# An attention stage's hand-written order: two query chunks moved ahead of an output projection, the first two heads' groups scored one step later

## The chip, the cores and the metric

One core of a Trainium2 chip. The metric is the device time of one execution in microseconds; the median of several runs counts. A difference under about 0.2% of it is small for the scatter of these runs.

## What is computed

One layer of a decoder trunk on 256 positions of 2048 features: a normalized input goes through one input projection; an SSD (Mamba-2) group and an attention group work side by side; one output projection adds both to the residual stream h; a gated feed-forward part and an embedding gate follow. The change lies in the attention group and in the output projection:

```python
a = rmsnorm(h)
z, xbc, dt, q, k, v = split(a @ W_in)          # 2048 -> 8224
...                                            # y_ssm from z, xbc, dt
qh, kh = rope(rmsnorm(q)), rope(rmsnorm(k))    # 32 query heads, 8 key heads of 64
for blk in blocks_of_128(positions):           # keys: this block and the one before
    sc = qh[blk] @ kh[blk-1:blk+1].T * 64**-0.5, masked to a window of 128
    m  = max(max(sc), sink)
    pr = exp(sc - m) / (sum(exp(sc - m)) + exp(sink - m))
    y_att[blk] = pr @ v[blk-1:blk+1]
h = h + concat(y_ssm, y_att) @ W_out           # 4096 -> 2048
h = h + (silu(g) * u) @ W_down                 # g, u from a causal convolution of rmsnorm(h) @ W_up
h = h + sigmoid(rmsnorm(h) @ W_pg) * rmsnorm(p @ W_pe)
```

## The kernel before

All large matrix products run in float32 accuracy from split operands: each weight tile `w` (128 x 2 x 512 floats) is loaded by SP's DMA queue, ScalarE (ACT) casts it to a rounded `wh` (L192), VectorE (DVE) subtracts to get the rest `wl` (L193), and TensorE (PE) makes three products for each 128-row piece: L222 (hi x wh), L223 (hi x wl), L224 (lo x wh). There are seven buffers of `w` and four each of `wh` and `wl`. One such tile with both blocks of 128 positions is 12 matmuls; this is one *step*, counted by `slot` in the attention stage.

In the attention stage (L638 to L839) the order of PE's instructions is written out by hand; the other engines' queues are ordered by a planner that follows the program order and a simulated time. The parts are:

- `chunk(c, then)` (L791): one chunk of 512 columns of the input projection, 8 steps. After the last, `then` takes the accumulator: `keys` for chunk 10, `load_v` for chunk 11, `queries(j, ...)` for chunk 12 + j, named `q(j)`.
- `queries(j)` (L696): for each block of 128 positions, `norm_rope` (L663; ACT scales and squares, DVE reduces and multiplies, POOL takes the root and rotates), then `flipped` (L683): POOL copies the two 16-bit halves into `half` (L701), a transposing DMA on SP's queue writes `flip` (L688), POOL copies `flip` into the tile `qT` (L689). A `q(j)` holds the queries of 8 heads.
- `scores(j, b, kvs)` (L727): PE multiplies `qT` with `kT` into `sc` (L738), DVE adds the band mask (L742) and reduces to the maximum (L749), ACT takes the exponentials (L753), and the probabilities are divided (for block 0 by DVE, L763, for block 1 by ACT, L761) and transposed by the same `flipped` (ACT fills `half` at L765, POOL writes `s` at L689). Three calls serve one j: block 0, and block 1 for each of two key heads. `sc` has one buffer, `s1` (block 1) has three.
- `values(j)` (L769): PE multiplies probabilities and `v`; ACT and DVE split the result into a tile `y`, which becomes the left operand of `output(4 + j)`. `y` has three buffers.
- `output(i)` (L800): one 512-row piece of the output projection: four column groups of two steps. After each group DVE adds the two accumulators to h (`add_to_h`, L396). `output(1)` to `output(3)` serve the SSD group, 4 to 7 the attention group.

`half` and `flip` have two buffers each, `qT` has two for each block, and the accumulators two pairs. The dictionary `at` says after which step each call of scores and values is put; the tuple of parts (L823 to L833) says in what order the 8-step parts run. So the steps of the old order are: 0 to 7 keys, 8 to 15 q(0), 16 to 23 load_v, 24 to 31 q(1), 32 to 39 output(1), 40 to 47 q(2), 48 to 55 output(2), 56 to 63 q(3), 64 to 71 output(3), then output(4) to output(7) up to 103.

Of the kernel before, what the change touches and what calls it, by code (L numbers as in the profile page):

```python
# [65 lines left out]
def hybrid_layer(  # L66
# [54 lines left out]
    def acc_pair():  # L121
        return [ps_acc.tile([P, NC], F32, tag=f"acc{b}", name=nm(f"acc{b}")) for b in range(NB)]
# [17 lines left out]
    def load_first(k, pieces=1):  # L140

        xt = sb(xin, [P, T], "xt", bufs=6)
        nc.sync.dma_start(xt, xT[:, k, :])
        w = sb(wp, [P, KW, NC], "w", bufs=WR)
        n = KW // pieces
        for c in range(0, KW, n):
            cs = slice(c, c + n)
            nc.sync.dma_start(w[:, cs, :], w_in[cs, k // KW, :, (k % KW) * NC : (k % KW + 1) * NC].rearrange("c p n -> p c n"))
        return w, xt

    first = [load_first(0, KW), load_first(1, KW)]
# [46 lines left out]
    def load_w(src, kt=KW, pieces=1):  # L198

        w = sb(wp, [P, KW, NC], "w", bufs=WR)  # L200
        wh = sb(wp, [P, KW, NC], "wh", F32R)
        wl = sb(wp, [P, KW, NC], "wl", F32R)
        n = kt * NC // pieces
        w2, wh2, wl2 = (t.rearrange("p a b -> p (a b)") for t in (w, wh, wl))
        for i in range(pieces):
            s = slice(i * n, (i + 1) * n)
            nc.sync.dma_start(w2[:, s], src[:, s])
            split(w2[:, s], wh2[:, s], wl2[:, s])
        return wh, wl

    def products(acc, lhs, w, k0, kt, total, apart=False, halves=False, whole=None):

        wh, wl = w
        order = [(i, b) for i in range(kt) for b in range(NB)]
        if apart:
            order.sort(key=lambda ib: ib[1])
        if halves:
            order = order[:kt]
        for i, b in order:
            k = k0 + i  # L220
            hi, lo = lhs(k, b)
            PE.matmul(acc[b], lhsT=hi, rhs=wh[:, i, :], start=(k == 0), stop=False)  # L222
            PE.matmul(acc[b], lhsT=hi, rhs=wl[:, i, :], start=False, stop=False)  # L223
            PE.matmul(acc[b], lhsT=lo, rhs=wh[:, i, :], start=False, stop=(k == total - 1 or (b == NB - 1 and k + 1 == whole)))  # L224
        if halves:
            b = NB - 1
            for c in range(0, NC, NC // 2):
                cs = slice(c, c + NC // 2)
                for i in range(kt):
                    hi, lo = lhs(k0 + i, b)  # L230
                    for left, right in ((hi, wh), (hi, wl), (lo, wh)):
                        PE.matmul(
                            acc[b][:, cs],
                            lhsT=left,
                            rhs=right[:, i, cs],
                            start=False,
                            stop=True,
                            skip_group_check=True,
                        )
# [8 lines left out]
    class Lhs:  # L248
# [8 lines left out]
        def part(self, k):  # L257
            h, l = self.t[k // KG]
            return h[:, k % KG, :], l[:, k % KG, :]
# [133 lines left out]
    def add_to_h(acc, n):  # L393
        for b in range(NB):
            hs = hres[b][:, n * NC : (n + 1) * NC]
            V.tensor_tensor(out=hs, in0=hs, in1=acc[b], op=ALU.add)  # L396
# [241 lines left out]
    with tc.tile_pool(name="att_s", bufs=2) as as_, tc.tile_pool(name="att", bufs=2, reuse_waits="tile") as ap_, tc.tile_pool(name="ps_sc", bufs=1, space=PSUM) as ps_sc:  # L638
# [57 lines left out]
        def queries(j, acc):  # L696
            qTs[j] = []
            for b in range(NB):
                n = norm_rope(acc, b, qrope)
                qT = sb(ap_, [P, 4, P], f"qT{b}")  # L700
                flipped(qT, NC, lambda half: G.tensor_copy(half, halves(n)))  # L701
                qTs[j].append(qT)
# [66 lines left out]
        def values(j):  # L769

            yT = Lhs(yp_, KG, "y")
            for b in range(NB):
                o = tr_tile()
                for kv in range(2):
                    pT = probs.pop((j, b, kv))
                    vs = slice((2 * j + kv) * HD, (2 * j + kv + 1) * HD)
                    for kb in range(b + 1):
                        for e in range(2):
                            PE.matmul(  # L779
                                v3(o[e * HD : (e + 1) * HD, kv * 2 * P : (kv + 1) * 2 * P], 2),  # L780
                                lhsT=v[kb][:, vs],
                                rhs=pT[e][:, :, kb, :],
                                start=(kb == 0),
                                stop=(kb == b),
                                skip_group_check=True,
                            )
                hi, lo = (t[:, :, b * P : (b + 1) * P] for t in yT.t[0])
                split(v3(o, 4), hi, lo)
            held[4 + j] = (yT, w_out, 4 + j, 1)

        def chunk(c, then):  # L791
            acc = acc_pair()
            n = KT // KW
            for s in range(n):
                products(acc, aT, load_w(w_in[c, s]), s * KW, KW, KT, s == n - 1)
                if s == n - 1:
                    then(acc)
                yield

        def output(i):  # L800
            lhs, w, i0, ni = held.pop(i)
            for n in range(4):
                acc = acc_pair()
                for s in range(2):
                    products(acc, lhs, load_w(w[i0 * 2 + s, n]), s * KW, KW, KG, s == 1)
                    if s == 1:
                        add_to_h(acc, n)
                    yield

        at = {}  # L810
        for j, first, value in ((0, (28, 31, 34), 48), (1, (43, 46, 50), 64), (2, (58, 61, 65), 79), (3, (75, 77, 80), 93)):
            for n, (b, kvs) in zip(first, ((0, (0, 1)), (1, (0,)), (1, (1,)))):
                at[n] = lambda j=j, b=b, kvs=kvs: scores(j, b, kvs)
            at[value] = lambda j=j: values(j)
# [3 lines left out]
        def q(j):  # L818
            return chunk(12 + j, lambda acc: queries(j, acc))

        slot = 0
        with tc.manual_schedule(engines={PE.engine}):
            for part in (  # L823
                lambda: chunk(10, keys),
                lambda: q(0),
                lambda: chunk(11, load_v),
                lambda: q(1),
                lambda: output(1),
                lambda: q(2),
                lambda: output(2),  # L830
                lambda: q(3),
                *(lambda i=i: output(i) for i in range(3, 8)),
            ):  # L833
                for _ in part():
                    if slot in at:
                        at[slot]()
                    slot += 1
# [163 lines left out]
```

## Time and profile before

| | us |
|---|---|
| runs | 1432.59, 1432.73, 1434.25 |
| median | 1432.73 |
| the profiled execution | 1436.61 |
| its span, first to last instruction | 1434.9 |
| PE busy | 1423.2 (99%) |
| DVE busy | 984.1 (69%) |
| ACT busy | 804.2 (56%) |
| POOL busy | 286.2 (20%) |

The profile gives each engine's busy time, the idle time before each instruction with what ended it, and a timeline. A matmul's record is longer than the distance to the next matmul's start, so neighbouring records overlap, and holes are read from the starts. The granted TensorE clock is full (1.00) for the whole span.

### The profile page before, as it was taken

The numbers are of one execution on the slowest core, as the hardware profiler recorded it, in microseconds if no ns is written. First come the engines' busy times: TensorE is split into PE (matmuls) and PEld (weight loads), VectorE is DVE, ScalarE is ACT, GpSimd is POOL, SyncE is SP. The second block draws the span as 40 slices with busy tenths as digits, with TensorE's granted clock in tenths as the row PEclk, the third lists the DMA queues.
The fourth block names the chain that finished last, engine by engine and source line by source line (L and its number), as shares of the span: only waits on it lengthen the run. The fifth ranks groups of instructions, "written<-read, shape, count | busy, mean of one in ns | idle before, by whom it ended". The sixth has DMA issues, their size and how long they took to land.

```text
span 1434.9 us, 18092 instructions
## 1 busy us (share of the span) xinstructions
PE 1423.2 (99%) x6527; PEld 1167.3 (81%) x6527; DVE 984.1 (69%) x1242; ACT 804.2 (56%) x1101; POOL 286.2 (20%) x212
## 2 busy tenths in 40 slices
PE   9999999999999999999999999999999999999998
PEld 7887888888787778888888888888888888888887
DVE  6678876776678897656667646765675576476854
ACT  6675555644567666556556446545554554455643
POOL 0002010008345432013243112201320131120000
PEclk9999999999999999999999999999999999999999
DMA  9656656548687778577887767867876877776671
GB/s 332 236 173 198 215 177 185 171 148 223 188 220 187 209 220 220 168 211 207 219 226 202 217 205 206 225 196 198 230 208 192 223 201 218 206 208 190 208 226 65
DMA packets 163467, 292.62 MB, mean 204 GB/s; under 512 B 93041, under 2 KB 95921, under 8 KB 162993
## 3 DMA queue, kind: packets, MB, share of 16 engines
q1 hardware_dynamic: 162944, 290.99, 70.5%
q8 instruction: 51, 0.84, 0.2%
q10 hardware_dynamic: 432, 0.48, 0.1%
q14 instruction: 40, 0.32, 0.1%
HBM read 268.32 MB, written 2.13 MB: 188 GB/s over the span
## 4 chain that ended last, share of the span: by engine, by line
PE 68%; DVE 1%; ACT 0%; issue 0%; POOL 0%; DVEq 0%; ACTq 0%
PE acc L222 22%; PE acc L224 22%; PE acc L223 22%; PE tr L779 1%; PE tr L272 0%; PE sc L738 0%; DVE wl L193 0%; ACT s L753 0%; DVE nm L749 0%; DVE s L742 0%; ACT wh L192 0%; DVE sg L931 0%; ACT s L761 0%; DVE qkr L672 0%; DVE h L396 0%
## 5 line engine op out<-in xcount | busy, mean ns | idle before, releaser
L193 DVE TENSOR_TENSOR wl<-w,wh 128x1024 fp32r<-128x1024 f32 (+1 forms) x495 | 634.9, 1288 | 378.5 <-ACT wh L192 376.4
L192 ACT CAST wh<-w 128x1024 fp32r<-128x1024 f32 (+1 forms) x495 | 514.8, 1045 | 480.7 <-PE acc L224 431.4
L223 PE MATMUL acc<-wl,ah 128*128 128x512 f32 x1278 | 500.1, 391 | 1.5 <-DVE wl L193 1.5
L224 PE MATMUL acc<-wh,al 128*128 128x512 f32 x1278 | 499.0, 391 | 0.0
L222 PE MATMUL acc<-wh,ah 128*128 128x512 f32 x1278 | 498.3, 392 | 0.0
L223 PEld LDWEIGHTS acc<-wl,ah 128*128 128x128 f32 x1278 | 240.1, 188 | 52.3 <-DVE wl L193 2.4
L222 PEld LDWEIGHTS acc<-wh,ah 128*128 128x128 f32 x1278 | 240.1, 188 | 51.0 <-issue 1.4
L224 PEld LDWEIGHTS acc<-wh,al 128*128 128x128 f32 x1278 | 240.1, 188 | 50.1 <-issue 0.7
L224 PE MATMUL acc<-wh,gl 128*128 128x512 f32 x352 | 137.1, 390 | 0.0
L223 PE MATMUL acc<-wl,gh 128*128 128x512 f32 x352 | 137.1, 390 | 0.0
L222 PE MATMUL acc<-wh,gh 128*128 128x512 f32 x352 | 136.5, 390 | 0.0
L881 POOL COPY half<-u 128x1024 uint16<-128x1024 uint16 x44 | 62.0, 1422 | 264.3 <-ACT u L879 264.3
L222 PE MATMUL acc<-wh,yh 128*128 128x512 f32 x256 | 101.6, 397 | 0.6 <-DVE h L396 0.6
L223 PE MATMUL acc<-wl,yh 128*128 128x512 f32 x256 | 99.9, 390 | 0.0
L224 PE MATMUL acc<-wh,yl 128*128 128x512 f32 x256 | 99.7, 390 | 0.0
L884 POOL COPY uc<-flip 128x1024 uint16<-128x1024 uint16 x44 | 54.9, 1248 | 177.2 <-DMA flip<-half 174.9
L223 PEld LDWEIGHTS acc<-wl,gh 128*128 128x128 f32 x352 | 66.1, 188 | 13.7
L224 PEld LDWEIGHTS acc<-wh,gl 128*128 128x128 f32 x352 | 66.1, 188 | 13.6
L222 PEld LDWEIGHTS acc<-wh,gh 128*128 128x128 f32 x352 | 66.1, 188 | 13.6
L288 DVE SCALAR_TENSOR_TENSOR cv<-uc,fcw,cv 128x254 f32<-128x254 f32 (+1 forms) x176 | 73.2, 476 | 3.4 <-ACT cv L286 3.4
L396 DVE TENSOR_TENSOR h<-h,acc 128x512 f32<-128x512 f32 x112 | 73.0, 678 | 1.8 <-PE acc L224 1.8
L222 PEld LDWEIGHTS acc<-wh,yh 128*128 128x128 f32 x256 | 48.1, 188 | 14.6 <-issue 2.0
(239 smaller groups left out, 1129.2 us busy)
## 6 DMA issues: line engine op xcount, KB each, us to landing
w<-in_w_up_dram SPq DMA_DIRECT2D x176, 512.0 KB, 4.2
w<-in_w_in_dram SPq DMA_DIRECT2D x126, 512.0 KB, 4.2
w<-in_w_down_dram SPq DMA_DIRECT2D x88, 512.0 KB, 4.3
w<-in_w_out_dram SPq DMA_DIRECT2D x64, 512.0 KB, 4.2
w<-in_w_pg_dram SPq DMA_DIRECT2D x32, 512.0 KB, 4.3
seg<-scr SPq DMA_DIRECT2D x8, 512.0 KB, 5.0
xt<-in_xT_dram SPq DMA_DIRECT2D x16, 128.0 KB, 7.0
h<-in_x_dram SPq DMA_DIRECT2D x2, 1024.0 KB, 8.7
```

The lines of the kernel that those rows point to most:

```text
L192: S.copy(hi, src)
L193: V.tensor_tensor(out=lo, in0=src, in1=hi.bitcast(F32), op=ALU.subtract)
L222: PE.matmul(acc[b], lhsT=hi, rhs=wh[:, i, :], start=(k == 0), stop=False)
L223: PE.matmul(acc[b], lhsT=hi, rhs=wl[:, i, :], start=False, stop=False)
L224: PE.matmul(acc[b], lhsT=lo, rhs=wh[:, i, :], start=False, stop=(k == total - 1 or (b == NB - 1 and k + 1 == whole)))
L288: V.scalar_tensor_tensor(out=dst[:, s:], in0=ps[:, : T - s], scalar=taps[n - 1 - s], in1=dst[:, s:], op0=ALU.mult, op1=ALU.add)
L396: V.tensor_tensor(out=hs, in0=hs, in1=acc[b], op=ALU.add)
L779: PE.matmul(v3(o[e * HD : (e + 1) * HD, kv * 2 * P : (kv + 1) * 2 * P], 2), lhsT=v[kb][:, vs], rhs=pT[e][:, :, kb, :], start=(kb == 0), st ...
L881: G.tensor_copy(half.rearrange("p (a n) -> p a n", a=2), u_.bitcast(U16).rearrange("p (n a) -> p a n", a=2))
L884: G.tensor_copy(uc[:, :, b * P : (b + 1) * P].bitcast(U16).rearrange("p f (t a) -> p f t a", a=2), flip.rearrange("p (a f) t -> p f t a", ...
```

## The change

The order of the parts is altered: `q(2)` runs ahead of `output(1)` and `q(3)` ahead of `output(2)`; before, each ran behind it. The steps after which scores and values are put are altered with it.

```diff
-        for j, first, value in ((0, (28, 31, 34), 48), (1, (43, 46, 50), 64), (2, (58, 61, 65), 79), (3, (75, 77, 80), 93)):
+        for j, first, value in ((0, (29, 32, 35), 49), (1, (44, 47, 51), 65), (2, (58, 61, 66), 79), (3, (73, 75, 80), 93)):
...
                 lambda: q(1),
+                lambda: q(2),
                 lambda: output(1),
-                lambda: q(2),
-                lambda: output(2),
                 lambda: q(3),
-                *(lambda i=i: output(i) for i in range(3, 8)),
+                *(lambda i=i: output(i) for i in range(2, 8)),
```

In the new order q(2) has the steps 32 to 39, output(1) 40 to 47, q(3) 48 to 55 and output(2) 56 to 63; the rest stands as it was.

## Rows read from the trace of the kernel before

**Rows 1.** Page, busy us (share of the span) and instructions of each engine.
```profile
PE 1423.2 (99%) x6527; PEld 1167.3 (81%) x6527; DVE 984.1 (69%) x1242; ACT 804.2 (56%) x1101; POOL 286.2 (20%) x212
```

**Rows 2.** Waits of PE, whole run: who waited for whom, us, times, longest.
```profile
PE sc L738 <- POOL qT L689: 2.6, 2, 1.4
...
PE acc L222 <- DVE h L396: 0.6, 1, 0.6
```

**Rows 3.** Timeline of PE, steps 28 and 31: start us, us, instruction, [idle before <-releaser].
```profile
369.51 0.39 PE L224 MATMUL acc<-wh,al 128*128 128x512 f32 x1
...
370.19 0.39 PE L224 MATMUL acc<-wh,al 128*128 128x512 f32 x1
371.95 0.60 PE L738 MATMUL sc<-kT,qT 64*128 64x128 f32 x6 [1.37 <-POOL qT L689]
...
381.13 0.39 PE L224 MATMUL acc<-wh,al 128*128 128x512 f32 x1
381.44 1.13 PE L738 MATMUL sc<-kT,qT 64*128 64x256 f32 x8
```

**Rows 4.** Timeline of PE at the end of step 61.
```profile
474.61 0.39 PE L224 MATMUL acc<-wh,al 128*128 128x512 f32 x1
476.23 0.49 PE L738 MATMUL sc<-kT,qT 64*128 64x256 f32 x2 [1.24 <-POOL qT L689]
```

**Rows 5.** Timeline of PE in step 54, in output(2).
```profile
451.10 0.40 PE L224 MATMUL acc<-wh,yl 128*128 128x512 f32 x1
452.09 0.50 PE L222 MATMUL acc<-wh,yh 128*128 128x512 f32 x1 [0.59 <-DVE h L396]
```

**Rows 6.** Timeline of POOL, copies for queries(0) and queries(2) and one of scores.
```profile
370.75 1.15 POOL L689 COPY qT<-flip 128x1024 uint16<-128x1024 uint16 x1 [7.14 <-DMA flip<-half]
...
458.48 2.04 POOL L701 COPY half<-qkr 128x1024 uint16<-128x1024 uint16 x1
475.03 1.15 POOL L689 COPY qT<-flip 128x1024 uint16<-128x1024 uint16 x1 [14.51 <-PE acc L224]
476.80 2.91 POOL L689 COPY s<-flip 128x2048 uint16<-128x2048 uint16 x1 [0.62 <-DMA flip<-half]
```

**Rows 7.** Timeline of SP's DMA queue, 457 to 472 us.
```profile
459.65 9.34 SPq L207 DMA_DIRECT2D w<-in_w_out_dram  x5
469.08 5.55 SPq L688 DMA_TRANSPOSE flip<-half  x2
```

**Rows 8.** Groups of ACT, 356.8 to 560 us: count | busy, mean ns | idle before, releasers.
```profile
L765 ACT COPY half<-s 128x2048 uint16<-128x2048 uint16 x12 | 22.8, 1899 | 5.0 <-DMA flip<-half 2.8 <-DVE s L763 1.9 <-ACT wh L192 0.3
```

**Rows 9.** Timeline of DVE, steps 53 and 54, and at step 62.
```profile
450.23 1.21 DVE L749 TENSOR_REDUCE nm<-s 128x4 f32<-128x1024 f32 x1
451.36 0.67 DVE L396 TENSOR_TENSOR h<-h,acc 128x512 f32<-128x512 f32 x1
...
477.62 4.31 DVE L193 TENSOR_TENSOR wl<-w,wh 128x1024 fp32r<-128x1024 f32 x2
```

**Rows 10.** Windows: us, then busy of PE, PEld, DVE, ACT, POOL; output(1), q(2), output(2).
```profile
382.50:405.70 23.20, 23.20 (x107) 18.75 (x106) 21.80 (x30) 16.27 (x35) 14.16 (x13) 1.00 0.68 191
405.70:430.10 24.40, 24.40 (x122) 19.57 (x121) 16.29 (x20) 16.32 (x32) 7.95 (x4) 1.00 0.98 250
430.10:457.10 27.00, 26.41 (x130) 19.96 (x128) 24.32 (x33) 18.48 (x35) 15.18 (x13) 1.00 0.76 172
```

**Rows 11.** Groups of DVE, 356.8 to 560 us, columns as in rows 8.
```profile
L742 DVE TENSOR_TENSOR s<-sc,band 128x1024 f32<-128x1024 f32 x12 | 14.6, 1215 | 0.2 <-PE sc L738 0.2
...
L763 DVE TENSOR_TENSOR s<-s,den 128x1024 f32<-128x1024 f32 x4 | 4.9, 1222 | 0.1
```

**Rows 12.** Timeline of DVE, weight casts for the steps 57 and 58.
```profile
458.34 1.28 DVE L193 TENSOR_TENSOR wl<-w,wh 128x1024 fp32r<-128x1024 f32 x1 [0.75 <-ACT wh L192]
...
460.66 1.21 DVE L193 TENSOR_TENSOR wl<-w,wh 128x1024 fp32r<-128x1024 f32 x1
```

**Rows 13.** Timeline of PE, first matmul of step 57 that reads wl.
```profile
460.14 0.39 PE L223 MATMUL acc<-wl,ah 128*128 128x512 f32 x1
```

## The prediction

> **What bounds the kernel now.** I read the page first. TensorE (PE) is the engine that sets the time: it is busy for 99% of the span [rows 1]. A busy share of 99% still hides short holes, because a matmul's record (0.39 us) is longer than the distance to the next one's start (three take 0.68 us, so 0.227 each) [rows 3]. So the second view is the list of what PE waited for in the whole run. Only two entries lie in the attention stage that the change touches: 2.6 us in two waits of score matmuls for qT, and 0.6 us in one wait of an output-projection matmul for an addition to h [rows 2]. The third view is PE's timeline at these three places. It says how long each hole is from start to start, and this is what the change can give back. A step (12 matmuls) takes 12 x 0.227 = 2.72 us.
>
> The first hole is ahead of the first scores (step 28): 370.19 to 371.95 is 1.76 us, where the same hand-over three steps later (381.13 to 381.44) takes 0.31, so 1.45 us are lost [rows 3]. The second is ahead of the third query chunk's second scores (step 61): 474.61 to 476.23, 1.62 us, so 1.31 are lost [rows 4]. The third is in output(2), step 54: 0.99 us where 0.23 is usual, so 0.76 are lost [rows 5].
>
> The rule of the Trainium skill, "Perfetto Trace Analysis", section "Tensor Engine Instruction", is that a matmul's recorded end is modelled and not observed. The idle times of the rows (1.37, 1.24, 0.59) come from such ends and would put the first two holes at 2.61 us; start to start gives 2.76. I use the starts.
>
> **The change, part by part.** *First scores one step later (28 to 29, 31 to 32, 34 to 35).* Their qT copy ends at 370.75 + 1.15 = 371.90 [rows 6]. Queries(0) and everything in program order ahead of step 28 stay where they are, so I leave that time alone. The scores would now start at 370.19 + 2.72 + 0.31 = 373.22, with 1.3 us to spare. The hole of 1.45 us goes. What is late next is the second block's qT for step 32, which also gets one step more.
>
> *Third query chunk q(2) one output sooner (its last step goes from 47 to 39).* Its scores stay at 58 and 61. Today the second block's 16-bit copy is done at 458.48 + 2.04 = 460.52, but qT is copied only at 475.03 [rows 6]. The time between goes on SP's queue: five weight loads stand ahead of the two transposing DMAs, which are issued from 469.08 [rows 7]. Those loads cannot be passed; but 8 steps more (21.8 us) stand against a shortage of 1.31 us, so even an equally slow path is in time. This hole goes too. The sum so far is 1.45 + 1.31 = 2.76 us.
>
> *Fourth query chunk q(3) one output sooner (63 to 55), its scores at 73 and 75 (75 and 77 before).* It had no wait before and gets 6 steps more. Gain 0. What it costs is that all that queries() issues comes earlier: per chunk four ACT operations, six on VectorE (DVE), fourteen on POOL, and two transposing DMAs on SP. They go ahead of 8 weight loads on SP and 8 pairs of weight casts on ACT and DVE. The matmuls and weight loads of q and output only swap places, and are of equal size; PE's work is unchanged.
>
> *Values one step later (48 to 49, 64 to 65), scores 65 to 66.* values(0) writes the y buffer that output(1) reads, and output(1) now ends at step 47 rather than 39. Step 48 lies between, so this costs nothing; if that cover went, ACT's split would wait for the rest of a step, at most 2.72 us, and no matmul needs it before output(4). scores at 66 take the buffer that values(1) frees at 65, the same distance of one step as before. values(2) stays at 79, so its last scores have 13 steps rather than 14; there is no wait to judge from, so it is bounded by 0 and 2.72 us. I take 0, as the rows show no wait of a value matmul at 14 [rows 2].
>
> *A shared buffer.* The 16-bit copies of queries and scores rotate through two buffers. The scores at 44 and 47 now follow queries(2), and those at 58 and 61 follow queries(3), so ACT may have to wait for a transposing DMA. The nearest row: 2.8 us of such waiting in twelve copies, none of it followed by a PE wait [rows 8, 2]. Bounds 0 and 2.8; I take 0.
>
> *DVE, stage by stage.* This is where the third hole comes from, and it may come back. In output(2) the reduction of a score (450.23) sits on DVE's queue between the two additions to h, and the second addition starts at 451.36 and frees the accumulator at 452.03 [rows 9]. DVE is busy 21.80 of 23.20 us in output(1), 24.32 of 27.00 in output(2), but only 16.29 of 24.40 in q(2) [rows 10]. From the durations a block-1 score costs DVE 1.22 us for the band [rows 11] and 1.21 for the reduction [rows 9], 2.43 together, and a block-0 score 1.22 more for its multiplication [rows 11]; the small operations are left out on both sides. After the change output(1) follows queries(2) and holds one block-0 score in place of two block-1 scores: 21.80 - 4.86 + 3.65 = 20.6 us, in 23.2 less one score's 1.2 on PE, 22.0. Output(2) follows queries(3) and holds a block-0 and a block-1 score, where the old output(1) held two block-1: 21.80 + 1.22 = 23.0 in 23.2. So output(1) gets easier, and output(2) stays as tight as the old output(1), which had no wait, and tighter than the old output(2), which had one. I can't read from this whether the wait for h returns. Its price is between 0 and a few times 0.76; I take one such wait of the same size, because output(2) remains the stage with the least room. So nothing is gained on that hole: sum 2.76 us.
>
> **How the sum stands to the runs.** The profiled execution took 1436.61 us (span 1434.9), 3.9 above the median of 1432.73. Taking 2.76 off gives 1433.9 for a profiled execution and 1430.0 for the median. The holes might be a little shorter in an execution without the profiler; no row shows that.
>
> **Rivals.** *B: the third hole goes as well.* For it: the scores at 50 and the values at 48, which crowded DVE beside the additions, are no longer in output(2); output(1) gets lighter. Against it: 23.0 of 23.2. It gives 2.76 + 0.76 = 3.52 us less, 1429.2.
>
> *C: output(2) becomes DVE-bound, and the kernel ends slower.* Place: steps 56 to 63. There the weight casts run just ahead of PE: in the old run at the same steps a cast ended at 458.34 + 1.28 = 459.62 and the matmul that reads it started at 460.14, a lead of 0.52 us [rows 12, 13]. Price: two casts that started at 477.62 beside a POOL copy (476.80 for 2.91) took 4.31 us, where two at 1.21 take 2.42; 1.9 are lost [rows 6, 9, 12]. Moving queries(3) next to this stage puts four more POOL copies there. From a lead below 1.9 each such meeting stops PE for what is left. One or two of them give 1430.0 + 1.9 to 1430.0 + 3.8, 1431.9 to 1433.8. Three or more fully uncovered, 5.7 us and up, give 1435.7 or more: slower by over 0.2%. Against it: the total load on the stage before it (q(3), by the row of q(2)) leaves DVE 8 us to get ahead again, and the old output(1) met the same copies without a wait.
>
> The Trainium skill speaks against the change here: "SBUF — State Buffer", section "SBUF: two separate sides", calls the port pair that DVE and GpSimd share an exclusive lock, held for a whole instruction. The two casts above agree with it: the first would start when the POOL copy ends. By it alone rival C would be likelier than I make it.
>
> *D: the change doesn't reach the first wait.* The planner that orders SP's queue could put the transposing DMA one weight load later; qT would then be ready at 371.90 + 2.72 = 374.62, 1.4 after the scores could start, and the gain falls to 1.36: 1431.4. Against it: nothing ahead of step 28 in program order is altered.
>
> **How the numbers follow.** Forecast A (two holes gone, one stays), 1430.0: 0.40, its own range 1429.6 to 1430.4. B, 1429.2: 0.36. C: 0.12 for 1431.9 to 1433.8, and 0.07 for 1435.7 and more. D, 1431.4: 0.05. About 0.2% (2.87 us, so 1429.86 and 1435.60) is what a measurement here can tell from no change. B and a fifth of A are faster: 0.44. C's upper part is slower: 0.07. The rest, 0.49, is within. For 8 in 10 the range runs from 1428.9, a little under B, to 1432.9, which takes in D and half of C's lower part; C's upper half and a rest are left out.
>
> **What would show it.** In the new trace PE's list of waits should have no score matmul waiting for qT, with the hand-over at step 29 at 0.3 us; the second qT copy of the third chunk should end tens of us ahead of its scores. A wait for h, if any, should lie in steps 56 to 66. The forecast is wrong if PE waits for wl there (C), if the qT wait is still there (D), or if a hole opens outside the attention stage, which this reasoning leaves at zero.

## The result, and the profile after

| | before | after |
|---|---|---|
| median, us | 1433.63 (1432.59 to 1434.69, 8 runs) | 1437.69 (1437.09 to 1440.27, 8 runs) |
| the profiled execution, us | 1436.61 | 1437.09 |
| the attention stage in it, us | 312.47 | 314.77 |
| granted clock, mean of the span | 1.000 | 0.998 |

The ratio is 1.0032, with a 95% interval of 1.0021 to 1.0042: the change makes the kernel 4.06 us slower, where the forecast had it 2.7 us faster. The attention stage is counted here and below in the profiled execution from the last matmul of the SSD part to the last transposition of h, start to start; behind it both traces take the same time (817.94 and 817.93 us). Ahead of it the profiled execution of before lost 1.3 us more at weight casts than the one of after, and its stage began 1.8 us later. So the two profiled executions differ by 0.5 us only, the stage by 2.3, and the medians by 4.1; the 1.8 between the last two are not accounted for by one profile of each.

The engines' busy times, as in [rows 1], show nothing of it:

```profile
PE 1424.0 (99%) x6527; PEld 1167.3 (81%) x6527; DVE 984.1 (69%) x1242; ACT 803.8 (56%) x1101; POOL 282.3 (20%) x212
```

The waits of PE after, as in [rows 2]: no score matmul waits for qT any more. New is the first line, 3.4 us of waiting for ACT's copies of the accumulators of the queries (L665); the wait for h is still there.

```profile
PE acc L222 <- ACT qkr L665: 3.4, 2, 2.8
...
PE acc L222 <- DVE h L396: 0.5, 1, 0.5
```

PE's timeline after (start us, us, instruction, idle before and its releaser), at the first scores (step 29), then in output(1), steps 41 and 42, then at the start of step 58 in output(2), then in step 70 in output(3):

```profile
371.12 0.39 PE L224 MATMUL acc<-wh,al 128*128 128x512 f32 x1
371.44 1.16 PE L738 MATMUL sc<-kT,qT 64*128 64x128 f32 x16
...
408.33 0.39 PE L224 MATMUL acc<-wh,yl 128*128 128x512 f32 x1
411.47 0.63 PE L222 MATMUL acc<-wh,yh 128*128 128x512 f32 x1 [2.75 <-ACT qkr L665]
411.90 0.63 PE L223 MATMUL acc<-wl,yh 128*128 128x512 f32 x1
...
414.46 0.63 PE L223 MATMUL acc<-wl,yh 128*128 128x512 f32 x1
414.89 0.50 PE L224 MATMUL acc<-wh,yl 128*128 128x512 f32 x1
415.22 0.39 PE L222 MATMUL acc<-wh,yh 128*128 128x512 f32 x1
...
462.68 0.39 PE L224 MATMUL acc<-wh,yl 128*128 128x512 f32 x1
463.71 0.50 PE L222 MATMUL acc<-wh,yh 128*128 128x512 f32 x1 [0.65 <-ACT qkr L665]
...
504.77 0.50 PE L222 MATMUL acc<-wh,yh 128*128 128x512 f32 x1 [0.50 <-DVE h L396]
```

The first pair is the hand-over that took 1.76 us [rows 3]; it takes 0.32. The second hole [rows 4] is gone as well. In their place PE stands still at step 42 from 408.33 to 411.47, 3.14 us, of which 0.23 are usual: 2.91 lost. Behind that hole matmuls start 0.43 us apart (411.47, 411.90) rather than 0.227, which is half the rate: up to 415.22 there are eight such distances and one of 0.33, so 8 x 0.20 + 0.10 = 1.7 us more. At step 58 another 0.80 are lost (1.03 less 0.23), at step 70 0.66 in a wait for h. The sum is 2.91 + 1.7 + 0.80 + 0.66 - 1.45 - 1.31 - 0.76 = +2.55 us, against 2.30 measured for the stage.

What held the accumulator is seen on ACT's timeline after. The two copies L665, of q(2)'s two blocks, lie 3.8 us apart:

```profile
405.29 1.71 ACT L761 ACTIVATE s<-s,den 128x256 f32<-128x256 f32 x4 [0.76 <-DVE den L758]
406.91 0.67 ACT L665 ACTIVATE qkr<-acc,rx 128x512 f32<-128x512 f32 x1
407.48 1.89 ACT L765 COPY half<-s 128x2048 uint16<-128x2048 uint16 x1
409.27 1.04 ACT L192 CAST wh<-w 128x1024 fp32r<-128x1024 f32 x1
410.21 0.63 ACT L667 ACTIVATE hsq<-qkr 128x512 f32<-128x512 f32 x1
410.74 0.67 ACT L665 ACTIVATE qkr<-acc,rx 128x512 f32<-128x512 f32 x1
```

In the kernel before the two copies of q(1) and the two of q(2) follow each other closely:

```profile
382.84 1.26 ACT L665 ACTIVATE qkr<-acc,rx 128x512 f32<-128x512 f32 x2
...
432.04 0.68 ACT L665 ACTIVATE qkr<-acc,rx 128x512 f32<-128x512 f32 x1
432.74 0.63 ACT L667 ACTIVATE hsq<-qkr 128x512 f32<-128x512 f32 x1
433.28 0.67 ACT L665 ACTIVATE qkr<-acc,rx 128x512 f32<-128x512 f32 x1
```

Output(1) uses q(2)'s pair of accumulators for its second column group, from step 42 on. After the change PE could have gone on there at 408.56, and the second copy ends at 411.41. From 405.29 ACT has work without a pause until then: the division and the 16-bit copy of a block-1 score, a weight cast, a square. The windows after, q(2) and output(1) (columns as in [rows 10], the last three being granted clock, DMA share and GB/s; the third stretch lies in the second):

```profile
378.10:402.40 24.30, 24.30 (x113) 19.24 (x112) 20.35 (x26) 18.10 (x43) 11.19 (x8) 1.00 0.61 152
402.40:430.20 27.80, 25.05 (x113) 19.80 (x112) 23.27 (x26) 17.73 (x23) 20.18 (x21) 0.94 0.89 227
405.00:416.00 11.00, 8.25 (x30) 6.34 (x29) 7.58 (x10) 10.41 (x14) 5.00 (x4) 0.84 0.90 201
```

Over a whole stage ACT is busy 18.10 of 24.30 and 17.73 of 27.80 us, which looks like room; in the 11 us from 405 it is busy 10.41. But this share by itself doesn't make PE wait: in the kernel before ACT is busy for the whole 11 us from 376. The granted clock is 0.84 in the 11 us from 405.

### The profile page after: what moved, and what is told of

Read it like the earlier page. It is cut to its first block, busy times and chain, and to the rows that moved or that the text cites. A ratio compares the mean times of both kernels' runs of the same rounds, so it can differ in the third digit from the quotient of the medians.

```text
span 1435.3 us, 18092 instructions
## 1 busy us (share of the span) xinstructions
PE 1424.0 (99%) x6527; PEld 1167.3 (81%) x6527; DVE 984.1 (69%) x1242; ACT 803.8 (56%) x1101; POOL 282.3 (20%) x212
## 4 chain that ended last, share of the span: by engine, by line
PE 64%; DVE 0%; ACT 0%; issue 0%; DVEq 0%
PE acc L222 21%; PE acc L223 21%; PE acc L224 21%; PE tr L272 0%; PE tr L779 0%; PE sc L738 0%; DVE sg L930 0%; DVE wl L193 0%; DVE nm L749 0%; DVE s L742 0%; DVE sg L931 0%; ACT wh L192 0%; ACT s L761 0%; DVE h L396 0%; ACT sg L929 0%
```

## The experiments

Each group of experiments was timed beside the kernel before on one chip; rows with the same time under "before" are one group, and rows of different groups are compared by their distance from it. How far one schedule scatters between groups is seen at e15, which only moves tiles of after in memory: it is 3.0 us above its before, where after is 4.06 above. A difference of 1 us between groups is therefore not read. Stage is the attention stage of one profiled execution.

| | median, us | before | ratio (95%) | stage, us |
|---|---|---|---|---|
| before | | | | 312.47 |
| after | 1437.69 | 1433.63 | 1.0032 (1.0021 to 1.0042) | 314.77 |
| e1 scores of j = 0 later, alone | 1431.55 | 1433.95 | 0.9981 (0.9973 to 0.9990) | 309.53 |
| e2 after, those scores early | 1436.19 | 1433.95 | 1.0017 (1.0008 to 1.0025) | 313.97 |
| e3 q(2) moved, q(3) not | 1438.43 | 1433.95 | 1.0030 (1.0019 to 1.0041) | 317.23 |
| e4 q(3) moved, q(2) not | 1431.83 | 1433.95 | 0.9991 (0.9979 to 1.0002) | 310.40 |
| e12 e4, last scores later | 1432.02 | 1434.42 | 0.9983 (0.9974 to 0.9992) | 311.42 |
| e6 scores of j = 0 and 2 later | 1432.99 | 1434.17 | 0.9992 (0.9983 to 1.0001) | 310.82 |
| e7 before, a hole made | 1436.79 | 1434.17 | 1.0017 (1.0008 to 1.0026) | 314.56 |
| e5 after, third accumulator pair | 1435.50 | 1434.17 | 1.0008 (1.0000 to 1.0017) | 313.99 |
| e8 after, one copy by DVE | 1436.54 | 1434.17 | 1.0013 (1.0004 to 1.0022) | 314.53 |
| e10 after, a division left out | 1435.97 | 1434.42 | 1.0013 (1.0004 to 1.0022) | 313.96 |
| e11 after, a division without its wait | 1438.88 | 1434.42 | 1.0031 (1.0019 to 1.0042) | 317.00 |
| e13 e8 and e10 together | 1438.12 | 1434.51 | 1.0027 (1.0017 to 1.0038) | 314.43 |
| e14 after, three buffers qkr | 1437.16 | 1434.09 | 1.0019 (1.0011 to 1.0028) | 314.12 |
| e15 the room of e14 alone | 1437.09 | 1434.09 | 1.0020 (1.0011 to 1.0029) | 313.71 |
| e16 e14 and e5 together | 1437.46 | 1434.09 | 1.0029 (1.0019 to 1.0038) | 314.26 |
| e17 after, half of q(2)'s casts | 1433.40 | 1434.43 | 0.9994 (0.9985 to 1.0003) | 311.33 |
| e18 e1, half of q(2)'s casts | 1431.71 | 1434.43 | 0.9980 (0.9971 to 0.9989) | 308.56 |

### Which part of the change costs

**e1**, on the kernel before:

```diff
-        for j, first, value in ((0, (28, 31, 34), 48), ...
+        for j, first, value in ((0, (29, 32, 35), 49), ...
```

> The old order of parts, only the first head group's scores one step later (29, 32, 35) and its values at 49. Theory 'release': what costs time in the changed kernel is that output(1) needs the accumulators of q(2) back while ACT still works off scores, so with the parts in the old order nothing of that is paid and only the 1.45 us hole ahead of the first scores goes: 1432.2 us against 1433.6, no half-clock matmuls. Theory 'scores': the later scores themselves (the last of them at 35 instead of 34) are what holds ACT up; then a hole of some 3 us opens in output(1), and the time is 1435 or more.

Measured: 2.4 us faster. PE's waits in the stage are one for h and none for qT: the second hole went too, though q(2) stayed where it was. The new order of the scores changed SP's queue ahead of step 61: four weight loads stand ahead of the two transposing DMAs there (issued from 463.71), not five as in [rows 7].

```profile
PE acc L222 <- DVE h L396: 0.7, 1, 0.7
```

**e2**, on the kernel after: the row of j = 0 as `(0, (28, 31, 34), 49)`.

> The changed kernel with the first head group's scores back at 28, 31, 34. Theory 'release' with the scores as the thing that holds ACT: the copies of q(2)'s accumulators come one step (2.72 us) earlier relative to step 42, so of its 2.91 us hole about 0.2 is left and the half-clock matmuls (1.8 us) go; the hole of 1.45 us at step 28 is back: 1437.7 - 2.7 - 1.8 + 1.45 = 1434.6 us. Theory 'DVE': DVE is the bound in output(1) whatever the scores' place, so the hole stays near 2.9 and 1.45 is added: 1439.

Measured: 1436.19, still 2.2 above before, so the move of the parts costs by itself. But it is not worse than after, as an additive account wants: the qT hole is 1.12, the hole at step 42 only 0.95, and no matmul behind it runs at half rate. Neither expected time came out: the hole at step 42 shrank as theory 'release' had it, but holes of 1.27 us at step 58 and of 0.70 to 1.09 at the steps 64 and 70 are there as well. I read the small hole as the scores being off ACT's queue a step earlier; it wasn't tried apart.

**e3**, on the kernel after: q(3) behind output(2) again, and the row of j = 3 as before.

> Only q(2) is moved ahead of output(1); q(3) stands behind output(2) as in the old order, with its scores at 75, 77, 80. Theory 'release': the hole at step 42 and the half-clock matmuls after it stay (2.9 + 1.8 us), the smaller hole at step 58 (0.8 us) goes: 1436.9. Theory 'clock' (the slow matmuls are not tied to that hole but to the whole run's activity): they fall elsewhere or not at all.

**e4**, on the kernel after:

```diff
                 lambda: q(1),
-                lambda: q(2),
                 lambda: output(1),
+                lambda: q(2),
                 lambda: q(3),
```

> Only q(3) is moved ahead of output(2); q(2) stands behind output(1) as in the old order, so q(2) and q(3) follow each other; scores and values as in the changed kernel. Theory 'release': no scores chain stands ahead of the copies of q(2)'s accumulators before an output (the next part is q(3), whose first two groups of 8 steps use the other pair first), so no hole at 42 and no half-clock matmuls; a hole of up to 1 us behind q(3) at step 58: 1437.7 - 4.7 = 1433.0. Theory 'DVE': output(2), with queries(3) and two scores, is the heaviest stage and shows the hole: 1436 or more.

**e12**, on e4: the row of j = 3 as `(3, (75, 77, 80), 93)`, as before.

> The kernel with only q(3) moved, and the last head group's scores back at 75 and 77. With the scores at 73 and 75 the weight casts were only 0.1 us ahead of PE at step 73 and three small holes of 0.3 us followed. If those come from the earlier scores, they go: 1431.8 - 0.9 = 1430.9 us. If q(3) ahead of output(2) is what costs there, the time stays at 1431.8 or more.

Measured: with q(2) moved the kernel is 4.5 us slower and has the hole at step 42 (3.27 us, and some eight matmuls at half rate behind it). That is 1.5 above the expectation: the hole at step 58 is gone, but PE stands 1.64 us at step 57 for a weight cast. With only q(3) moved the median is 2.1 lower (the interval just reaches 1), and no place in the stage loses more than 0.34 us; e12 is 2.4 faster. The step from e4 to e12 was expected to give 0.9, and the runs don't show it: a wait for h has grown to a hole of 2.14 us at step 72. So by the medians, against the kernel before: the scores of j = 0 later give 2.4 (e1), q(3) moved on top of it about nothing, and q(2) moved takes some 6 (+4.06 after, -2.1 e4). The whole loss comes from q(2), and the gain expected of it was to be had without it. The parts don't simply add, though: the later scores gain 2.4 in the old order and nothing in the new one (e2 is 2.2 above its before, after 4.06 and e15 3.0 above theirs).

**e6**, on the kernel before: `(0, (29, 32, 35), 49)` and `(2, (59, 62, 66), 79)`.

> The old order of parts; first head group's scores one step later (29, 32, 35; values 49) and the third's one step later (59, 62, 66). Both holes that the prediction counted are then closed without moving a chunk. By the prediction's own sum 1434.0 - 1.45 - 1.31 = 1431.2 us; no PE wait for qT, one wait for h of about 0.7 us left. If the holes are not worth their length in executions without the profiler, it stays at 1432 or more, near the kernel that shifts the first scores alone (1431.6).

Measured: 1.2 lower, an interval that reaches 1, and less than e1. A new wait for qT of 1.6 us opens at step 77, for the fourth chunk. One step later isn't better for each of them.

### What a hole costs

**e7**, on the kernel before: the first scores one step earlier, `(0, (27, 31, 34), 48)`.

> The old kernel with its first scores put after step 27, one step too early, so that the hole ahead of them grows by a step: 1.45 + 2.72 = 4.2 us; nothing else is moved. Theory 'clock follows the hole': the matmuls behind it run at half clock (0.43 us apart instead of 0.23) for some ten matmuls, about 1.8 us, so the cost is 2.72 + 1.8 = 4.5 us: 1438.5. Theory 'clock is something else' (the run's activity as a whole): no slow matmuls there, cost 2.7 us less what is caught up: 1436.7 or less.

PE's timeline of e7, and the window behind the hole (columns as above):

```profile
365.62 0.39 PE L224 MATMUL acc<-wh,al 128*128 128x512 f32 x1
369.57 2.08 PE L738 MATMUL sc<-kT,qT 64*128 64x128 f32 x16 [3.57 <-POOL qT L689]
...
372.60 0.63 PE L224 MATMUL acc<-wh,al 128*128 128x512 f32 x1
...
375.42 0.40 PE L222 MATMUL acc<-wh,ah 128*128 128x512 f32 x1
...
372.00:376.00 4.00, 4.00 (x12) 3.09 (x12) 2.48 (x4) 1.58 (x9) 0.32 (x1) 0.60 0.39 57
```

The same matmul, the tenth behind the scores, in the kernel before, where the scores start at 371.95 [rows 3]:

```profile
375.23 0.39 PE L222 MATMUL acc<-wh,ah 128*128 128x512 f32 x1
```

One hole of 3.95 us, so 3.95 - 0.31 = 3.64 lost, is the only one in the stage of e7; the three of before, 1.45 + 1.31 + 0.76 = 3.52 together, are not there. By the holes alone the stage would be 0.1 us longer. It is 2.1 longer (314.56 and 312.47), and the median 2.6. What the slower clock cost is read from the first score to the tenth matmul behind it: 5.85 us (369.57 to 375.42) where before takes 3.28 (371.95 to 375.23), so 2.6 us; the smaller delays elsewhere in the stage must be some 0.6 less. The first scores took 2.08 us where they take 1.16 after, eight matmuls behind them stand 0.43 us apart, and the granted clock is 0.60 there. So slow matmuls can follow a hole that ACT had no part in: here PE waited for POOL. The median alone would not have shown it: it came out at the expectation without the clock, because two other holes closed that I had left in place.

### Which wait, and whether it is one

**e5**, on the kernel after: output(1) doesn't reuse q(2)'s pair, but takes two free banks for its second column group.

```diff
-                acc = acc_pair()
+                acc = [tr_tile(), tr_tile()] if i == 1 and n == 1 else acc_pair()
```

> The changed kernel, but output(1) takes its second accumulator pair from two transposing banks that are idle there, so that its steps 42 and 43 don't need the accumulators of q(2). The queues of the other engines keep their order. Theory 'release': the hole of 2.9 us at step 42 goes, and with it the nine half-clock matmuls (1.8 us); what is left of the lateness shows at step 44 or not at all: 1437.7 - 4.7 = 1433.0 us, 1434 if a rest of 1 us stays. Theory 'DVE' (weights or additions to h are late there anyway): PE waits for wl or h at nearly the same place, and the time stays over 1436.

**e8**, on the kernel after: block 1 of q(2) and q(3) is copied by DVE.

```diff
-            S.activation(out=r, in_=acc[b], func=AF.Copy, scale=rx[:, b : b + 1])
+            if by_dve:
+                V.tensor_scalar_mul(r, acc[b], rx[:, b : b + 1])
+            else:
+                S.activation(out=r, in_=acc[b], func=AF.Copy, scale=rx[:, b : b + 1])
```

> The changed kernel, but the accumulator of block 1 of q(2) and q(3) is copied by DVE instead of ACT. Theory 'release by ACT': DVE stands idle for 3.2 us at the place of the hole, so the accumulator is free before step 42 needs it; the hole of 2.9 us and the half-clock matmuls go, and the smaller hole behind q(3) (0.8) too: 1437.7 - 4.7 - 0.8 = 1432.2 us, up to 1433 if DVE's own work shifts. Theory 'DVE': the added work on DVE makes the stage worse, 1438 or more.

Measured: e5 is 1.3 us above its before and e8 2.4, where after is 4.06 above its own and e15 3.0; both were expected to give nearly all. In both the hole at step 42 is gone and no matmul runs at half rate. In e5 PE waits for the weight casts instead, one step later, at step 43. Its waits of PE, PE's timeline and DVE's:

```profile
PE acc L223 <- DVE wl L193: 1.0, 4, 0.4
PE acc L222 <- ACT qkr L665: 0.9, 1, 0.9
PE tr L223 <- DVE wl L193: 0.8, 1, 0.8
```

```profile
411.43 0.49 PE L222 MATMUL tr<-wh,yh 128*128 128x512 f32 x1
412.69 0.50 PE L223 MATMUL tr<-wl,yh 128*128 128x512 f32 x1 [0.77 <-DVE wl L193]
```

```profile
411.41 1.23 DVE L193 TENSOR_TENSOR wl<-w,wh 128x1024 fp32r<-128x1024 f32 x1 [4.02 <-ACT wh L192]
```

DVE itself was idle for 4.02 us ahead of that cast: ACT hadn't made `wh`. In e8 the casts are the larger part (first line, over the whole run; 2.4 of it in the stage); the second line is the copy of q(3)'s block 0, which ACT still makes, at step 58:

```profile
PE acc L223 <- DVE wl L193: 3.0, 5, 1.0
PE acc L222 <- ACT qkr L668: 1.2, 1, 1.2
```

So there are two walls, one step apart, and both lead to ACT's queue. The trace after has the second one already: the lead of the casts, from the end of `wl` to the first matmul that reads it, falls from 2.9 us at step 39 to 1.1, 0.6 and 1.0 at the steps 40 to 42. In the kernel before it is 2.2 at step 40 and 4.1 at step 42.

**e10**, on the kernel after (the division of j = 0, block 1, is left out):

```diff
-            if b:
+            if b and j == 0:
+                pass
+            elif b:
```

> The changed kernel without the division of the first head group's block-1 probabilities: eight ACT operations of 0.49 us (3.9 us, and the waits for DVE's denominators ahead of them) are left out between steps 32 and 41, so that part of the attention output is not normalized. Theory 'ACT backlog' (queries(1), two block-1 scores and queries(2) pile up on ACT's queue, and both the accumulators' copies and the weight casts come late for it): the copies come 4 us or more earlier, the hole at step 42 and the half-clock matmuls go, and the weight casts are not late either: 1437.7 - 4.7 = 1433.0 us or less. Theory 'DVE': DVE's work is unchanged, so at most the accumulators' hole turns into waits for wl, as with the third pair: 1435.5.

**e11**, on the kernel after: the same division is made with a constant column rather than `den`, so that ACT needn't wait for DVE's reciprocal; the work stays.

> The changed kernel with the same eight divisions on ACT, but by a constant column instead of DVE's denominator, so that ACT does the same work and no longer stands still for DVE there (4.3 us of waiting in two places); the output of those heads is scaled wrongly. If ACT's standing still behind DVE is what makes the copies late, this gains as much as leaving the divisions out: 1433.0 us. If ACT's work as such is too much, the hole stays: 1436 to 1437.7.

Measured: e10 gains a little (1435.97, 1.6 above its before) and keeps a hole of 2.39 us; e11 nothing (1438.88, a hole of 2.32). Both have seven matmuls at half rate behind it. ACT's pauses for `den` (4.3 us in two places in the trace after) are not the cause by themselves: that rival falls with e11. In e10 part of the time that ACT saved went into a wait for a `half` buffer (1.59 us for the transposing DMA), between the two copies. Another part went into a wait for DVE: ACT's exponentials of the last block-1 score start at 400.46 after and at 400.37 in e10, and ACT has stood still for 5.57 us there.

```profile
400.37 0.51 ACT L753 ACTIVATE s<-s,nm 128x256 f32<-128x256 f32 x1 [5.57 <-DVE nm L750]
```

So ACT's work alone is not the whole cause. In the trace after, ACT waits 6.9 us for DVE between 379.5 and 411.3, and DVE in turn waits 6.4 us for ACT's casts; the two engines form one chain. ACT's waits there:

```profile
ACT s L761 <- DVE den L758: 4.3, 2, 3.6
ACT s L753 <- DVE nm L750: 2.6, 2, 2.1
```

**e13**, on the kernel after: the edits of e8 and e10 together.

> Both reliefs at once in the changed kernel: block 1's accumulator of q(2) and q(3) copied by DVE, and the first head group's block-1 probabilities not divided (part of the attention output is not normalized). Theory 'two walls' (late accumulators, and behind them weight casts late because ACT and DVE are behind with their work at steps 36 to 43): each relief alone gained 1.2 to 1.7 us because the other wall then held PE; together they take away all that moving q(2) cost, about 6 us: 1432 us, with no hole over 0.5 us and no half-clock matmuls in steps 40 to 44. If one of the two is not a cause, the time stays near the better single one, 1436; if something else holds PE there, a hole with another releaser shows.

```profile
PE acc L223 <- DVE wl L193: 2.2, 3, 1.3
PE acc L222 <- DVE qkr L666: 2.0, 1, 2.0
```

Missed by 6 us: the copy on DVE stands behind the sum of squares of block 0, which waits for ACT's squares, and these stand behind a 16-bit copy that waits 1.67 us for `half`. DVE was made to wait for ACT.

**e14**, on the kernel after, with room taken from a lead tile (480 to 352 columns); **e15** is that room alone, **e16** e14 with e5.

```diff
-            r = sb(ap_, [P, NC], "qkr")
+            r = sb(ap_, [P, NC], "qkr", bufs=3)
```

> The changed kernel with three buffers instead of two for the tile qkr, into which ACT copies a query chunk's accumulators (512 bytes are taken from an unused tile at the start to make room). With two, the copies of q(2), which now follow those of q(1) by 8 steps, need the buffers that queries(1) still works in, and on ACT's queue a copy of probabilities, a weight cast and a square stand between the two copies (3.3 us). Theory 'qkr': with a third buffer the second copy comes two operations earlier, about 1.5 us, so the hole at step 42 halves to 1.4 and the half-clock matmuls (1.8 us) go: 1437.7 - 3.3 = 1434.4 us. Theory 'backlog' (ACT and DVE are behind whatever the buffers): weight casts hold PE there instead, as with the third accumulator pair, and it stays at 1435.5 or more.

> The control for the three qkr buffers: the changed kernel with only the unused tile at the start cut by 512 bytes, so that all later tiles lie 512 bytes lower. All theories: the same as the changed kernel, 1437.7 us with the hole at step 42 and the half-clock matmuls; if it differs by over 1 us, places in memory matter and the run with three buffers is read against this one.

> Three qkr buffers and the third accumulator pair for output(1) together: neither the accumulators nor qkr can hold anything at step 42. Theory 'backlog': what is left is ACT's and DVE's lateness itself: PE waits for wl at steps 40 to 43 by 1 to 2 us, no half-clock matmuls, 1435 us. Theory 'qkr': the casts are late only for the order that the buffers force, so no hole over 0.5 us is left there: 1433 us or less.

Measured: e14 is at 1437.16, its control e15 at 1437.09: the third buffer is worth nothing. It did what it was to do, the second copy stands directly behind the 16-bit copy and the hole falls to 1.79 us, but PE waits for the weight casts instead, at the steps 41, 54 and 57:

```profile
PE acc L223 <- DVE wl L193: 1.9, 3, 1.3
PE acc L222 <- ACT qkr L665: 1.4, 1, 1.4
PE acc L222 <- DVE h L396: 0.7, 1, 0.7
```

With e5's pair added (e16) the wait at step 42 is gone and no matmul runs at half rate, but PE still waits for weight casts at step 43 (1.26 us from start to start) and step 57, and for a copy at step 58 (1.60). At 1437.46 it is no better, and 2.5 above what theory 'backlog' said. So the theory that the buffers of `qkr` hold it falls as well.

**e17**, on the kernel after: q(2) (c = 14) loads and casts only every second of its weight tiles and uses each twice, so ACT makes four casts of 1.0 us less, DVE four of 1.2 us less and SP four loads less for the steps 32 to 39. **e18** is e1 with the same, as the control.

```diff
+                if c != 14 or s % 2 == 0:
+                    w = load_w(w_in[c, s])
-                products(acc, aT, load_w(w_in[c, s]), s * KW, KW, KT, s == n - 1)
+                products(acc, aT, w, s * KW, KW, KT, s == n - 1)
```

> The changed kernel, but the chunk q(2) (steps 32 to 39) loads and casts only every second weight tile and uses it twice: four loads, four casts on ACT (4 x 1.04 us) and four subtractions on DVE (4 x 1.22 us) are left out, so that the third query chunk comes out wrong; PE's matmuls, the accumulators, the buffers and the scores stay. Theory 'backlog' (between the first chunk's queries and the second's, ACT and DVE have more work than the steps have time, and whatever is late first holds PE): with 4 us less on either engine PE waits for neither accumulators nor wl in steps 40 to 44, no half-clock matmuls: 1437.2 - 4.7 = 1432.5 us or less. Theory 'order' (the second copy sits behind other work whatever the load): the hole at step 42 stays over 1.5 us, 1435.5 or more.

> The same half of q(2)'s weight tiles left out in the kernel with the old order of parts and the first scores one step later, as a control: there q(2) has the steps 40 to 47 and PE waits for nothing in them, so the work left out should be worth little: 1431.5 us, at most 1 us less. If it gains 3 us or more, the gain of the other run is no proof for the backlog.

Measured: e17 takes 1433.40, 4.3 us less than after (by the distances from before 5.1, and 4.0 against e15), and its stage 3.4 less; 1433.40 is 0.9 above the expectation of theory 'backlog' and 2.1 below that of theory 'order'. e18 takes 1431.71 against e1's 1431.55: nothing by the medians, though the stage of its profiled execution is 1.0 shorter. At step 42 of e17 PE doesn't wait, and no matmul runs at half rate. Its waits of PE in the stage, and ACT's timeline:

```profile
PE acc L222 <- DVE h L396: 1.4, 2, 0.7
```

```profile
403.02 0.67 ACT L665 ACTIVATE qkr<-acc,rx 128x512 f32<-128x512 f32 x1
403.58 1.89 ACT L765 COPY half<-s 128x2048 uint16<-128x2048 uint16 x1
...
406.85 0.68 ACT L665 ACTIVATE qkr<-acc,rx 128x512 f32<-128x512 f32 x1
```

The order on ACT's queue is that of the trace after but for a cast and a square that swap places; the 16-bit copy still stands between the two copies, and they lie the same 3.8 us apart. Only all of it comes 3.9 us sooner (0.3 of this as the whole stage began sooner). So the order is not what makes them late: with less work in the steps ahead, nearly the same order is in time. The 3.9 us are not ACT's four casts added up, though 4 x 1.04 = 4.2 is near, as ACT waits 4.84 us for DVE in between. Of the 3.9 us 2.1 come from DVE, whose maximum (L750) is ready sooner (first line after, second e17), 1.0 from one cast less between the exponentials and the copy, and 0.8 from the wait for `den` that is gone:

```profile
400.15 0.28 DVE L750 TENSOR_TENSOR nm<-nm,nsink 128x4 f32<-128x4 f32 x1
...
398.07 0.28 DVE L750 TENSOR_TENSOR nm<-nm,nsink 128x4 f32<-128x4 f32 x1
```

Nor do four casts less make the move free: e17 is 1.7 us above e18, which ran beside it. Two waits for h at step 70 of e17 (the line above, two holes of 1.1 us) are not there in e18.

## Why the prediction was wrong

**The two holes at qT: both gone, one of them counted for an edit that it didn't need.** "First scores one step later" was to bring the hand-over to 0.31 us at 373.22; it is 0.32 (step 28 itself came 1.8 us sooner in the run after, as the start was shorter). "Third query chunk one output sooner" was to free the second hole, and it is gone, but e1 shows that it goes without that move, by another order of SP's queue. So this gain of 1.31 us is no gain of q(2)'s move over the first edit. The move closes the hole too: it is gone in e2, where the first scores are early. It is gone even in e7, where neither edit is made, so it hangs on how SP's queue comes out.

**The failed step: what moving q(2) costs.** I listed for q(3) what queries() issues sooner (four ACT operations, six on DVE, fourteen on POOL, two DMAs) and set it at nothing, and of q(2) I looked only at qT. The cover that I didn't name is the time in which ACT and DVE work off a chunk of queries. Before, output(1) lay between q(1) and q(2): in its 8 steps ACT did queries(1) and two block-1 scores, and copied q(2)'s accumulators 2.2 and 3.5 us after its last matmul had started (432.04 and 433.28, 429.83). After, q(2) takes those steps itself: its casts come in the same 8 steps as queries(1) and the scores, and right behind it output(1) needs both q(2)'s accumulators, from its third step, and casts at the usual rate. The copies then come at 406.91 and 410.74, 4.7 and 8.5 us after q(2)'s last matmul (402.21), and 3.9 us later than with four casts less (e17). The release of an accumulator by L665 stands in no line of my working.

**"DVE, stage by stage".** I reckoned DVE's load in output(1) down to 20.6 of 22.0 us and called the stage easier; it came out at 23.27 of 27.80. (The 22.0 was a slip: the new output(1) holds a score too, at step 44.) Load by stage was the wrong measure, and one engine the wrong object: what decided was a chain in which ACT and DVE wait for each other, through q(2)'s steps and the first of output(1), and at its end DVE stood idle for ACT (e5). ACT is busy 64 to 74% of these stages and 95% of the 11 us from 405, but it is busy for the whole of 11 us elsewhere without a wait of PE, so no share of busy time shows the lateness; the time of the copies does.

**Rival C named the kind and missed the place.** It had casts that run just ahead of PE, behind a chunk of queries, as the way to a slower kernel, but in output(2), by POOL's copies beside DVE's casts, and with 0.07. In output(2) the loss is 0.80 us, by the same late copies of accumulators, and e4 shows that q(3) ahead of output(2) costs next to nothing. Its mechanism, a DVE operation held up beside a POOL copy, is in the trace after, but in q(2)'s steps (see below). The rows for C (a lead of 0.52 us at step 57 [rows 12, 13]) showed how little the casts have in hand; I should have taken the lead at every step, and asked what follows on ACT.

**The price of a hole.** I took each hole at its own length. The hole of 3.14 us cost about 1.7 more in matmuls at half rate. That term was missing in every rival.

**The third hole**, which A left in place: a wait for h is there in the trace after, at step 70 rather than in 56 to 66, and of 0.66 where 0.76 was taken.

**What stays open.** The two `half` buffers serve scores and queries alike, and ACT waited 1.59 (e10) and 1.67 us (e13) for one at this place. How much of the backlog is this sharing wasn't tried apart from the rest. Nor do the runs show which single operation ahead of step 42 should go to have q(2) there at no cost; of those tried (a copy, a division, a wait, a buffer, a pair of accumulators) none was enough, and four casts took away the wait at step 42 but not all of the cost. Since these took work from ACT, DVE and SP together, they don't say how much of it was which engine's. One rival within the chain was not tried: in the trace after, a small addition on DVE takes 2.11 us beside a copy on POOL, where the same one takes 0.16 in e17 (third line), and ACT's division waits 3.56 us for the reciprocal of its result. In all other runs with q(2) ahead of output(1), e2 and e17 apart, DVE also loses 1.6 us or more in one operation at this place. No run keeps the casts and takes this meeting away.

```profile
393.81 2.11 DVE L757 TENSOR_TENSOR den<-den,es 128x4 f32<-128x4 f32 x1
392.80 3.10 POOL L689 COPY s<-flip 128x2048 uint16<-128x2048 uint16 x1 [6.21 <-ACT es L756]
...
390.42 0.16 DVE L757 TENSOR_TENSOR den<-den,es 128x4 f32<-128x4 f32 x1 [1.03 <-ACT es L756]
```

## What to carry to other kernels

Before a chunk of work is moved next to another, list everything that its followers wait for (its accumulators' release, not only its last product), and compare the helper engines' work in the few steps between with the time of these steps; busy shares, over a stage or over 11 us, don't show a pile-up of 4 us, and the time from the last matmul to the copies does. If taking away one wait gives little and another engine's wait stands there instead, suspect the load; taking away work, with a control on a kernel without the wait, tests it, but not which engine's work it is. The simplest edit, e1 (0.9981), and e12 (0.9983) beat both kernels: try each part of a change alone.

## What was not expected of the hardware

Holes of PE of 2.32 (e11), 2.39 (e10), 3.14 (after and e15), 3.27 (e3) and 3.95 us (e7) were followed by six to eight distances of 0.43 us between matmuls, with a granted clock of 0.59 to 0.60 over the 4 us behind it (after, e7), so most of it at the lower level of 1.2 GHz; this costs 1.4 (e10) to 2.6 us (e7) on top of the hole. Holes of 1.76 (before, [rows 3]), 2.02 (e6), 2.14 (e12) and 2.35 us (e13) were not, so length alone doesn't decide it in this range. The Trainium skill, "TensorE: Matmul & The Clock Gate", Part 1, says of the gate on TensorE's clock that it knows half and full rate alone and is set by how busy the engine has recently been; the two spacings, 0.43 and 0.227, agree with the two rates.
